# The adaLN modulation vector of a two-layer decoder step: four parts of 512 columns side by side, one set of transposes for four, and other places for the work

## The chip, the cores and the metric

The kernel runs on one core of one Trainium2 chip. The metric is the device time of one execution in microseconds (us): 1722.26 us as the median of 3 runs (1722.0 to 1723.0). One further execution was recorded by the profiler. It took 1719.56 us, and its span, from the first to the last instruction, is 1717.9 us.

## The reference, cut to what matters

One inference step of two layers: layer 0 mixes tokens by sparse attention (NSA), layer 1 by a Mamba-2 SSD scan. 512 prompt tokens and 8 sample tokens go through together, so that every activation has 520 columns. Before each mixer and each MLP there is an RMSNorm whose scale and shift, and behind it a gate, come from a conditioning vector; that is adaLN:

```python
def adaln(c, w, b):
    m = jax.nn.silu(c) @ w + b                      # c: 9 vectors of 1024, w: 1024 x 6144 per layer
    return jnp.split(m[:, None, :], 6, axis=-1)
def modulate(x, w, shift, scale):
    return rmsnorm(x, w) * (1.0 + scale) + shift

# layer i: mp = adaln(c, ada_w[i], ada_b[i])
xp = xp + mp[2] * mixer(modulate(xp, norm_w[i, 0], mp[0], mp[1]))
xp = xp + mp[5] * mlp(modulate(xp, norm_w[i, 1], mp[3], mp[4]))
```

So six pieces of 1024 numbers are wanted per layer: shift, scale and gate of the mixer, then shift, scale and gate of the MLP. All is float32.

## The kernel before, in words

All activations lie with the model dimension on the 128 partitions and the 520 tokens along the free dimension. A product of 128 output channels is 48 matmuls (8 blocks of the inner dimension, three products of split high and low halves, two halves of the columns). Its weight is one tile `w` of 128 x 1024 (512 KB), loaded by a DMA on SP's queue. ScalarE (ACT) copies it into the high half `wh` and VectorE (DVE) subtracts to get the low half; this pair is called the split of a weight here. `w` has 4 buffers, `wh` has 6. `make_plan` writes down the order in which all `w` tiles are loaded, and `get_raw` issues loads at most 4 tiles ahead of the one it hands out, so a load waits for the tile four places before it to be read.

The vector `m` of adaLN is 48 columns of 128 x 9 per layer. `ada(l, cg)` computes 4 of them, one group of 512 columns of `ada_w` (a "cg"; 12 per layer). It takes 8 matmuls: the stationary operand is the silu of the conditioning vectors, 128 x 32 per block of the inner dimension `kt`, the moving operand is a 128 x 512 block of `ada_w`, which is half of a `w` tile. A float32 matmul stands as two instructions in the trace, so these are 16 instructions. Block `kt` writes PSUM partitions `32 j` to `32 j + 32` with `j = kt % 4`: the eight blocks go round the array's four column groups, and each column group holds a partial sum of two blocks. ACT copies the 128 x 512 result (tile `ad`), four PE transposes turn it, a DVE reduce adds the four partial sums, and a DVE add puts in the bias.

Groups 0 to 3 of layer 0 are computed in `start`. The others are placed by tables:

- `attend`: groups 4 to 11 of layer 0 and 0 and 1 of layer 1. `attention` walks through 64 items (head pair, query block, head) and a tail of 6, and after each item asks a `Weaver` for `ATT_RATE` steps of other work: the sample tokens' attention (`sam_cmp`, four times `sam_branch`, `sam_fin`) and the `ada` generators, of which four stand inside a `sam_branch`, between the softmax and its transposes.
- `mlp` of layer 0: groups 3, 5, 6, 8, 9, 11 of layer 1, each run as a whole after a product named in `MLP_CGS`.
- `boundary`, between two stages: groups 2, 4 and 10. The eight matmuls stand where the norm's chain is waited for, and the reduce and the add are a `hook` in `modulated`.
- the last part of `ssd` (called the SSD's output stage here): group 7.

The output stage of `ssd` runs 8 output products `ssd_out(3, n)`, and after each one `out_fin` adds to the residual (DVE), squares (ACT) and sums the squares on GpSimd (POOL). Then the boundary to the second MLP begins: a sum over partitions by PE (`s<-c,st`), a square root, a broadcast by PE (`s<-c,r`), and the modulation.

PE, ACT, DVE, POOL and the DMA queues each run their instructions in a fixed order, which the framework's scheduler sets when the program is built.

Of the kernel before, what the change touches and what calls it, by code (L numbers as in the profile page):

```python
# [14 lines left out]
ALU = mybir.AluOpType  # L15
# [70 lines left out]
def host_inputs(x):  # L86
    c = np.ascontiguousarray
    a = {}
# [3 lines left out]
    a['ada_w'] = x['ada_w'].reshape(2, 4, 2, 128, 12, 512).transpose(0, 4, 1, 3, 2, 5).reshape(2, 12, 4, 128, 1024)  # L92
# [169 lines left out]
class Step:  # L262
# [196 lines left out]
    def load_ada(self, l, cg, whole=False):  # L459
        ws = []  # L460
        if whole:
            for kq in range(4):
                t = self.tile('wh', [128, 1024])
                self.load(t, self.I['ada_w'][l, cg, kq])
                ws += [t[:, 0:512], t[:, 512:1024]]
            return ws
        for kt in range(8):
            t = self.tile('h', [128, 512])
            self.load(t, self.I['ada_w'][l, cg, kt // 2, :, (kt % 2) * 512:(kt % 2 + 1) * 512])
            ws.append(t)  # L470
        return ws

    def ada(self, l, cg, tag='f', ws=None, fine=False):
# [18 lines left out]
        if fine:  # L492
            yield
# [80 lines left out]
    def boundary(self, tags, cg, ftag):  # L574

        ada = self.ada(1, cg, ftag, fine=True)
        for _ in range(8):
            next(ada)
        self.norm(tags, fill=ada)
        next(ada)  # L580
        h = self.modulated(lambda: next(ada))
        run_all(ada)
        return h

    def modulated(self, hook=None):
# [3 lines left out]
        for k in range(8):  # L589
            x = self.xa[k]  # L590
            self.tt(prompt(x), prompt(x), r, ALU.mult)
            if k == 0:
                self.tt(self.us, self.us, rs[:, None].to_broadcast([128, 8, 2, 4]), ALU.mult)
# [7 lines left out]
            if k == 0 and hook:  # L601
                hook()
# [519 lines left out]
    def sam_branch(self, br, k, ada):  # L1122
# [41 lines left out]
        yield from ada  # L1164
# [79 lines left out]
    def attend(self):  # L1244
        fill = [self.sam_cmp()]
        cgs = [(0, n) for n in range(4, 12)] + [(1, 0), (1, 1)]
        fill.append(self.ada(*cgs.pop(0)))
# [3 lines left out]
        fill += [self.ada(*c) for c in cgs]  # L1251
# [5 lines left out]
    def nsa_out(self):  # L1257
        h = [self.oh[i] for i in range(8)]
        self.norm_to(0, 1)
        for n in range(8):  # L1260
# [3 lines left out]
            self.scaled(n)  # L1264
        self.oh = {}
# [3 lines left out]
    def mlp(self, l, h, cgs, early=None):  # L1269
# [29 lines left out]
        for b in range(4):  # L1299
# [343 lines left out]
    def ssd(self, h):  # L1643
# [11 lines left out]
        for kind, n in SSD_SEQ:  # L1655
# [10 lines left out]
            elif kind == 'ada':  # L1666
                run_all(self.ada(1, n, 's'))
# [10 lines left out]
        fill = self.ada(1, OUT_CG, 's', fine=True)  # L1678
        for _ in range(8):
            next(fill)  # L1680
# [9 lines left out]
        run_all(fill)  # L1690
# [4 lines left out]
        self.ssd_out(3, range(2, 8))  # L1695
        self.yh = {}
        self.store(self.O['cv_p'], self.CP)
        self.store(self.O['cv_s'], self.SC)

# [44 lines left out]
    def make_plan(self):  # L1744
# [3 lines left out]
        def ada(l, *cgs):  # L1748
            for cg in cgs:
                E.extend(('ada', l, cg, k) for k in range(4))  # L1750
# [219 lines left out]
```

## Time and profile before

| | |
|---|---|
| median of 3 runs | 1722.26 us |
| the profiled execution | 1719.56 us |
| its span | 1717.9 us |
| PE busy | 1664.7 us, 97% of the span |
| DVE busy | 984.0 us, 57% |
| ACT busy | 761.6 us, 44% |
| DMA | 229.87 MB, 134 GB/s over the span |
| mean granted clock of PE | 0.993 |

The busy time of PE is the union of its matmuls; a matmul in flight counts even while the next one streams. The cost of a piece of PE work is therefore read from the timeline as the distance from its first start to the start of what follows. A view by windows gives the busy time of each engine in a stretch, the clock that was granted to PE there (1.00 is full speed, 0.50 half), and what the DMA engines moved. Of the stages, attention lies at about 208 to 431 us, the output product of the attention (`nsa_out`) at 431 to 480, the first MLP at 485 to 872, the SSD at 878 to 1333 with its output stage from about 1285, and the second MLP from 1333 to the end.

### The profile page before, as it was taken

To read this page: it belongs to the slowest core of one execution; us is meant where nothing else is said; L and a number is where in the kernel's file an instruction comes from. 1 tells how busy PE (TensorE), PEld (TensorE's weight loads), DVE (VectorE), ACT (ScalarE), POOL (GpSimd) and SP (SyncE) were. 2 spreads that over 40 slices of the span, in tenths; PEclk is the share of its full clock that TensorE was granted. 3 is DMA by queue.
4 is the path that set the end of the run, shared out by engine and by line. 5 is a ranking of instruction groups with operands and counts; after the bars stand their busy time and mean duration, and the time that the engine had idled before them with its cause. 6 is when DMAs were issued, how large, how long until landed. Compare 5 with 4: busy or idle time off the path is not lost.

```text
span 1717.9 us, 34708 instructions
## 1 busy us (share of the span) xinstructions
PE 1664.7 (97%) x13878; PEld 1538.2 (90%) x13878; DVE 984.0 (57%) x2423; ACT 761.6 (44%) x1624; POOL 143.5 (8%) x303
## 2 busy tenths in 40 slices
PE   7899999999999999999999999999998999999997
PEld 6699877667989999999989898899987999999997
DVE  2543377776464343433478968879797643434344
ACT  3534366666443131322456666646564422323231
POOL 2000112310001000000001102111022000000000
PEclk9999999999999999999999999999999999999999
DMA  8822656545433523333433442344324232323321
GB/s 302 288 87 99 215 195 223 169 148 196 137 126 97 184 87 135 99 135 136 136 135 102 135 166 90 117 135 138 125 89 160 74 99 87 96 90 93 93 86 51
DMA packets 72114, 229.87 MB, mean 134 GB/s; under 512 B 8770, under 2 KB 15218, under 8 KB 71186
## 3 DMA queue, kind: packets, MB, share of 16 engines
q1 hardware_dynamic: 62546, 198.45, 35.1%
q0 software_dynamic: 8832, 28.16, 4.5%
q8 instruction: 109, 1.79, 0.4%
q10 hardware_dynamic: 576, 1.05, 0.2%
q14 instruction: 51, 0.42, 0.1%
HBM read 204.02 MB, written 23.61 MB: 133 GB/s over the span
## 4 chain that ended last, share of the span: by engine, by line
PE 71%; DVE 8%; ACT 2%; issue 1%; POOLq 0%; DMA 0%; SPq 0%; POOL 0%; DVEq 0%; ACTq 0%
PE a L323 60%; PE s L323 5%; PE f L323 2%; PE o L323 1%; DVE wh L336 1%; PE sc L323 1%; PE t L327 1%; DVE c L345 1%; DVE g L345 1%; ACT wh L330 1%; DVE acc L336 1%; PE s L327 0%; DVE ss L1462 0%; PE f L327 0%; ACT h L333 0%
## 5 line engine op out<-in xcount | busy, mean ns | idle before, releaser
L323 PE MATMUL a<-h,wh 128*128 128x256 f32 x5952 | 743.4, 284 | 3.8 <-ACT t L333 1.6
L323 PEld LDWEIGHTS a<-h,wh 128*128 128x128 f32 x5952 | 723.3, 189 | 10.1 <-issue 3.7
L330 ACT ACTIVATE wh<-w 128x1024 fp32r<-128x1024 f32 x212 | 224.5, 1059 | 521.8 <-PE a L323 480.4
L336 DVE TENSOR_TENSOR wh<-w,wh 128x1024 fp32r<-128x1024 f32 x212 | 259.6, 1225 | 266.4 <-ACT wh L330 265.8
L323 PEld LDWEIGHTS a<-hid,wh 128*128 128x128 f32 x3072 | 370.2, 188 | 5.0 <-issue 4.2
L323 PE MATMUL a<-hid,wh 128*128 128x256 f32 (+1 forms) x3072 | 373.7, 283 | 0.0
L336 DVE TENSOR_TENSOR t<-a,c 128x8 f32<-128x8 f32 x72 | 12.0, 167 | 217.4 <-PE a L323 217.4
L323 PE MATMUL a<-yh,wh 128*128 128x256 f32 (+1 forms) x768 | 98.4, 285 | 3.0 <-DVE acc L336 1.5
L323 PEld LDWEIGHTS a<-yh,wh 128*128 128x128 f32 x768 | 93.7, 188 | 5.2 <-DVE acc L336 2.2
L330 ACT ACTIVATE hid<-t 128x520 fp32r<-128x520 f32 x64 | 40.9, 639 | 84.5 <-DVE t L336 84.5
L330 ACT ACTIVATE h<-t 128x128 f32<-128x128 f32 (+3 forms) x128 | 52.5, 440 | 46.5 <-PE t L327 46.3
L333 ACT ACTIVATE h<-sc,m 128x128 f32<-128x128 f32 (+3 forms) x128 | 66.6, 530 | 14.6 <-DVE m L340 12.5
L336 DVE TENSOR_TENSOR hid<-t,hid 128x520 fp32r<-128x520 f32 x64 | 44.7, 700 | 42.3 <-ACT hid L330 42.3
L327 PE MATMUL t<-c,h 128*128 128x128 f32 x320 | 53.5, 281 | 1.9 <-DVE h L340 0.7
L345 DVE SCALAR_TENSOR_TENSOR c<-a,c,c 128x512 f32<-128x512 f32 (+1 forms) x74 | 53.9, 728 | 1.8 <-PE a L323 1.8
L333 ACT ACTIVATE xb<-bc,x 128x128 f32<-128x128 f32 x128 | 46.4, 419 | 15.8 <-DVE xb L345 11.2
L323 PE MATMUL sc<-kv,q 128*128 128x128 f32 (+3 forms) x128 | 49.5, 387 | 0.0
L323 PEld LDWEIGHTS a<-q,wh 128*128 128x128 f32 x384 | 46.3, 188 | 1.0 <-ACT wh L330 0.8
L327 PEld LDWEIGHTS t<-c,h 128*128 128x128 f32 x320 | 34.4, 141 | 13.8 <-issue 7.7
L323 PE MATMUL a<-q,wh 128*128 128x256 f32 (+1 forms) x384 | 46.7, 283 | 0.0
L323 PE MATMUL sc<-kv,c 128*128 128x128 f32 (+3 forms) x128 | 42.3, 331 | 4.2 <-POOL c L947 4.2
L1462 DVE SCALAR_TENSOR_TENSOR ss<-ss,c,xb 128x128 f32<-128x128 f32 x128 | 43.3, 361 | 4.4 <-ACT xb L333 4.2
(366 smaller groups left out, 1941.9 us busy)
## 6 DMA issues: line engine op xcount, KB each, us to landing
w<-in_w_dram SPq DMA_DIRECT2D x128, 512.0 KB, 3.5
w<-in_ada_w_dram SPq DMA_DIRECT2D x80, 512.0 KB, 3.6
w<-in_w_ssd_dram SPq DMA_DIRECT2D x40, 512.0 KB, 3.6
w<-in_w_nsa_dram SPq DMA_DIRECT2D x20, 512.0 KB, 3.6
ss<-in_ssm_dram SPq DMA_DIRECT2D x16, 512.0 KB, 4.3
out_ssm_s_dram<-ss POOLq DMA_DIRECT2D x16, 512.0 KB, 3.0
w<-in_w_sout_dram SPq DMA_DIRECT2D x16, 512.0 KB, 4.1
cm<-in_cmp_dram SPq DMA_DIRECT2D x24, 256.0 KB, 4.0
```

Of the source, the lines that this page charges most:

```text
L323: self.nc.tensor.matmul(out, lhsT, rhs, start=start, stop=stop, skip_group_check=True)
L327: self.nc.tensor.transpose(out, in_, self.C('ident')[0:k, 0:k])
L330: self.nc.scalar.activation(out, in_, AF.Copy, **kw)
L333: self.nc.scalar.activation(out, in_, f, **kw)
L336: self.nc.vector.tensor_tensor(out, a, b, op=op)
L345: self.nc.vector.scalar_tensor_tensor(out, a, s, b, op0=op0, op1=op1, **kw)
L1462: self.nc.vector.scalar_tensor_tensor(out, a, s, b, op0=op0, op1=op1)
```

## The change: what it does

`ada` now takes two pairs of groups at once. The weight's layout in memory is changed, so that one `w` tile holds 1024 columns of one inner block `kt` (a pair of groups). For each `kt`, two tiles are fetched and four matmuls follow, one for each of four groups of 512 columns, each on a column group of its own; each column group accumulates all eight blocks. The copy to `ad` and the four transposes are done once for four groups, the reduce is gone, and the bias is added by two DVE adds that read the transposes from PSUM. `ada` stops after each `kt`, after the copy, after the transposes and at the end, 11 steps.

The places are new. In `attend` only layer 0 is left, two calls of four groups, between the branches, and `ATT_RATE` is 1.0 instead of 1.2. Layer 1's twelve groups are three calls: pairs 0 and 1 with one `kt` after each of the products 1 to 6 of `nsa_out` and the last two at the boundary to the first MLP; pairs 2 and 4 likewise over the last eight products of the first MLP and the boundary to the SSD; pairs 3 and 5 in the SSD's output stage (blocks 0 to 5) and the boundary to the second MLP. In that boundary pair 3 is the shift that the modulation adds, so `hook` stands earlier in `modulated`. The first four groups of layer 0 keep the old scheme as `ada_first`.

```diff
+    def ada(self, l, pairs, tag='f'):
         ps = self.tile(tag, [128, 512])
         for kt in range(8):
-            if ws is not None:
-                w = ws[kt]
-            else:
-                if kt % 2 == 0:
-                    raw = self.get_raw(('ada', l, cg, kt // 2))
-                w = raw[:, (kt % 2) * 512:(kt % 2 + 1) * 512]
-            j = kt % 4
-            self.mm(ps[32 * j:32 * j + 32], self.sc[:, kt, :], w, kt < 4, kt >= 4)
-            if fine or kt % 4 == 3:
-                yield
+            raw = [self.get_raw(('ada', l, a, kt)) for a in pairs]
+            for j in range(4):
+                self.mm(ps[32 * j:32 * j + 32], self.sc[:, kt, :], raw[j // 2][:, (j % 2) * 512:(j % 2 + 1) * 512],
+                        kt == 0, kt == 7)
+            yield
...
-        m = self.m[l][:, cg * 4:cg * 4 + 4, :]
-        self.nc.vector.tensor_reduce(m, p.rearrange("p t j c -> p t c j")[:, :, 0:9, :], AX.X, ALU.add)
-        b = self.adab[:, l, cg * 4:cg * 4 + 4]
-        self.tt(m, m, b[:, :, None].to_broadcast([128, 4, 9]), ALU.add)
+        yield
+        for n, a in enumerate(pairs):
+            b = self.adab[:, l, 8 * a:8 * a + 8].rearrange("p (j t) -> p t j", t=4)
+            self.tt(self.m[l][:, 8 * a:8 * a + 8, :].rearrange("p (j t) c -> p t j c", t=4),
+                    p[:, :, 2 * n:2 * n + 2, 0:9], b[:, :, :, None].to_broadcast([128, 4, 2, 9]), ALU.add)
...
-        for br, k in SAM_ORDER:
-            fill.append(self.sam_branch(br, k, self.ada(*cgs.pop(0))))
+        for (br, k), pairs in zip(SAM_ORDER, ((2, 4), (3, 5), None, None)):
+            if pairs:
+                fill.append(self.ada(0, pairs))
+            fill.append(self.sam_branch(br, k))
...
-                if (b, n) in cgs:
-                    run_all(self.ada(1, cgs[b, n]))
+                if ada and b == 3 and n in ADA_AT:
+                    next(ada)
...
-        fill = self.ada(1, OUT_CG, 's', fine=True)
-        for _ in range(8):
+        fill = self.ada(1, (3, 5), 's')
+        for _ in range(2):
             next(fill)
...
-        run_all(fill)
+        for _ in range(2):
+            next(fill)
...
-        self.ssd_out(3, range(2, 8))
+        for n in (2, 4, 6):
+            self.ssd_out(3, (n, n + 1))
+            if n < 6:
+                next(fill)
...
-MLP_CGS = {(0, 2): 3, (0, 6): 5, (1, 2): 6, (2, 2): 8, (2, 6): 9, (3, 3): 11}
+ADA_AT = {1: 0, 2: 1, 3: 2, 4: 3, 5: 4, 6: 5}
...
-ATT_RATE = 1.2
+ATT_RATE = 1.0
```

The order on PE in the first MLP before, at the first group there (`a` is a product's PSUM tile, `f` the adaLN sum, `w` its weight; a row with x2 is two matmuls):

```order
L323 MATMUL f_7721<-w_7544,c_101 32x512 x2
L323 MATMUL f_7721<-w_7603,c_101 32x512 x2
L323 MATMUL f_7721<-w_7662,c_101 32x512 x2
L323 MATMUL f_7721<-w_7722,c_101 32x512 x2
...
L327 MATMUL f_7740<-c_72,ad_7738 128x128 x4
```

And now, in `nsa_out`, at the first two of the six places:

```order
L323 MATMUL a_6213<-q_6102,wh_6138 128x264
L323 MATMUL f_6272<-w_6135,c_101 32x512 x2
L323 MATMUL f_6272<-w_6141,c_101 32x512 x2
L323 MATMUL a_6287<-q_2980,wh_6143 128x256
...
L323 MATMUL f_6272<-w_6273,c_101 32x512 x2
L323 MATMUL f_6272<-w_6275,c_101 32x512 x2
L323 MATMUL a_6360<-q_2980,wh_6209 128x256
```

Eight matmuls in one piece and four transposes became pieces of four matmuls, one after each product, with no transposes between products.

The order on PE in the SSD's output stage before, at the broadcast of the SSD's own norm (`s<-c,r`; `a` is a product's PSUM tile):

```order
L323 MATMUL a_16805<-yh_16239,wh_16604 128x264
L323 MATMUL a_16805<-yh_16238,wh_16605 128x256
L323 MATMUL s_16756<-c_72,r_16753 128x128 x4
L323 MATMUL s_16730<-c_72,r_16753 128x8
L327 MATMUL s_16767<-c_72,xd_16765 128x128 x4
L323 MATMUL a_16805<-yh_16238,wh_16605 128x264
L323 MATMUL a_16805<-yh_16488,wh_16604 128x256
```

And now, from the same broadcast to the sixth output product (`s_16561` is the adaLN sum):

```order
L323 MATMUL s_16596<-c_72,r_16593 128x128 x4
L323 MATMUL s_16570<-c_72,r_16593 128x8
L323 MATMUL s_16561<-w_16503,c_101 32x512
L323 MATMUL s_16561<-w_16505,c_101 32x512 x2
L323 MATMUL s_16561<-w_16507,c_101 32x512 x2
...
L323 MATMUL s_16561<-w_16509,c_101 32x512 x2
...
L323 MATMUL s_16561<-w_16515,c_101 32x512 x2
...
L323 MATMUL s_16561<-w_16517,c_101 32x512 x2
...
L323 MATMUL s_16561<-w_16718,c_101 32x512 x2
L323 MATMUL s_16561<-w_16720,c_101 32x512 x2
```

The four transposes gave way to blocks 2 to 5, and the scheduler has cut the blocks into unequal pieces between and within the products.

The order on DVE in the same stage before (`acc<-acc,a` takes a product in, `acc<-acc,z` scales it, `wh<-w,wh` is the low half of a weight's split):

```order
L336 TENSOR_TENSOR acc_12906<-acc_12906,a_16683 128x520
L336 TENSOR_TENSOR wh_16680<-w_16671,wh_16679 128x1024
L336 TENSOR_TENSOR acc_12933<-acc_12933,a_16684 128x520
L336 TENSOR_TENSOR wh_16802<-w_16673,wh_16801 128x1024
L495 TENSOR_REDUCE c_100<-s_16767 128x36
L336 TENSOR_TENSOR acc_12906<-acc_12906,z_16762 128x520
L336 TENSOR_TENSOR c_100<-c_100,c_88 128x36
...
L336 TENSOR_TENSOR wh_16882<-w_16675,wh_16881 128x1024
...
L336 TENSOR_TENSOR wh_16962<-w_16677,wh_16961 128x1024
```

And now:

```order
L336 TENSOR_TENSOR acc_12738<-acc_12738,a_16523 128x520
L336 TENSOR_TENSOR acc_12765<-acc_12765,a_16524 128x520
L336 TENSOR_TENSOR acc_12738<-acc_12738,z_16602 128x520
...
L336 TENSOR_TENSOR acc_12798<-acc_12798,a_16644 128x520
L336 TENSOR_TENSOR wh_16520<-w_16511,wh_16519 128x1024
...
L336 TENSOR_TENSOR wh_16641<-w_16513,wh_16640 128x1024
...
L336 TENSOR_TENSOR wh_16729<-w_16638,wh_16728 128x1024
...
L336 TENSOR_TENSOR wh_16817<-w_16726,wh_16816 128x1024
```

Before, two splits stood ahead of the scaling and two among the later products; now all four stand among the products, and the reduce and its add are gone from here.

## Rows read from the trace of the kernel before

**Rows 1.** The page, part 1: busy time, share of the span and instructions of each engine.

```profile
PE 1664.7 (97%) x13878; PEld 1538.2 (90%) x13878; DVE 984.0 (57%) x2423; ACT 761.6 (44%) x1624; POOL 143.5 (8%) x303
```

**Rows 2.** By windows: window, length, busy (instructions) of each engine, PE's clock, DMA share, GB/s.

```profile
34.00:64.00 30.00, 24.54 (x183) 15.35 (x182) 10.91 (x31) 11.91 (x19) 2.80 (x6) 1.00 0.99 357
...
209.00:345.00 136.00, 129.56 (x1227) 92.02 (x1226) 101.92 (x369) 87.02 (x279) 36.80 (x95) 0.99 0.59 202
345.00:420.00 75.00, 72.88 (x650) 51.06 (x650) 54.47 (x204) 48.95 (x157) 9.20 (x27) 1.00 0.46 167
...
440.00:480.00 40.00, 39.42 (x329) 37.77 (x327) 18.34 (x41) 16.23 (x23) 0.00 (x0) 1.00 0.32 93
...
485.00:872.00 387.00, 385.71 (x3207) 374.00 (x3205) 166.50 (x280) 124.96 (x167) 8.05 (x15) 1.00 0.37 122
```

**Rows 3.** Timeline of PE, first MLP: start, length, instructions.

```profile
561.35 1.92 PE L323 MATMUL f<-w,c 128*32 128x512 f32 x16
563.20 0.98 PE L323 MATMUL a<-hid,wh 128*128 128x256 f32 x6
564.02 0.65 PE L327 MATMUL f<-c,ad 128*128 128x128 f32 x4
564.43 22.60 PE L323 MATMUL a<-hid,wh 128*128 128x256 f32 x186
```

**Rows 4.** Timeline of PE, attention.

```profile
358.96 1.07 PE L323 MATMUL f<-w,c 128*32 128x512 f32 x8
359.95 0.44 PE L323 MATMUL sc<-kv,q 128*128 128x384 f32 x1
...
361.37 0.60 PE L327 MATMUL f<-c,ad 128*128 128x128 f32 x4
361.72 0.48 PE L323 MATMUL sc<-kv,q 128*128 128x512 f32 x1
```

**Rows 5.** By tile `ad`: one copy to it for each adaLN group outside the SSD.

```profile
L330 ACT ACTIVATE ad<-f x22: 572/598/616, 39.0 to 872.3; 128x512 f32<-128x512 f32 x22
```

**Rows 6.** Timeline of PE, SSD's output stage; in brackets idle time and who ended it.

```profile
1287.48 1.90 PE L323 MATMUL s<-w,c 128*32 128x512 f32 x10
1289.32 2.42 PE L323 MATMUL a<-yh,wh 128*128 128x256 f32 x18
1291.67 1.06 PE L323 MATMUL s<-w,c 128*32 128x512 f32 x6
1292.66 1.28 PE L323 MATMUL s<-c,yss 128*128 128x1 f32 x10
...
1311.59 5.98 PE L323 MATMUL a<-yh,wh 128*128 128x256 f32 x48 [1.44 <-DVE c L336]
...
1324.71 2.19 PE L323 MATMUL s<-c,st 128*128 128x1 f32 x10 [4.05 <-POOL st L534]
...
1333.22 14.50 PE L323 MATMUL a<-h,wh 128*128 128x256 f32 x96 [0.36 <-ACT h L333]
1348.40 11.79 PE L323 MATMUL a<-h,wh 128*128 128x256 f32 x96 [0.67 <-ACT t L333]
```

**Rows 7.** Timeline of DVE, the same stage.

```profile
1314.95 1.21 DVE L336 TENSOR_TENSOR wh<-w,wh 128x1024 fp32r<-128x1024 f32 x1
```

**Rows 8.** By windows, the same stage.

```profile
1320.00:1325.00 5.00, 0.95 (x6) 0.29 (x3) 4.93 (x10) 1.90 (x5) 3.08 (x2) 0.99 0.99 391
1325.00:1330.00 5.00, 4.42 (x21) 4.33 (x22) 0.28 (x2) 2.16 (x4) 0.00 (x0) 0.50 0.06 24
```

**Rows 9.** Timeline of PE, boundary between attention and first MLP.

```profile
480.02 1.28 PE L323 MATMUL t<-c,ssq 128*128 128x1 f32 x10 [0.60 <-DVE ssq L336]
...
484.57 0.63 PE L323 MATMUL a<-h,wh 128*128 128x256 f32 x3 [1.25 <-ACT h L333]
```

**Rows 10.** DMA issues: what, queue, count, KB each, median us from issue to landing.

```profile
w<-in_ada_w_dram SPq DMA_DIRECT2D x80, 512.0 KB, 3.6
...
wh<-in_ada_w_dram SPq DMA_DIRECT2D x4, 512.0 KB, 7.2
```

More of the change, by code (lines that the diff above doesn't have):

```diff
@@ L455, in first_products, with load_ada @@
         return ps
-    def load_ada(self, l, cg, whole=False):
+    def load_ada(self, cg, whole=False):
         ws = []
[L461 to L466, printed above, removed]
-        for kt in range(8):
-            t = self.tile('h', [128, 512])
-            self.load(t, self.I['ada_w'][l, cg, kt // 2, :, (kt % 2) * 512:(kt % 2 + 1) * 512])
+        for kt in range(8):
+            if not whole:
+                t = self.tile('h', [128, 512])
+            elif kt % 2:
+                t = u[:, 512:1024]
+            else:
+                u = self.tile('wh', [128, 1024])
+                t = u[:, 0:512]
+            self.load(t, self.I['ada_w'][0, cg // 2, kt, :, (cg % 2) * 512:(cg % 2 + 1) * 512])
@@ L470, in load_ada, with ada_first @@
             ws.append(t)
         return ws
-    def ada(self, l, cg, tag='f', ws=None, fine=False):
+    def ada_first(self, cg, ws):
+        ps = self.tile('f', [128, 512])
+        for kt in range(8):
+            j = kt % 4
+            self.mm(ps[32 * j:32 * j + 32], self.sc[:, kt, :], ws[kt], kt < 4, kt >= 4)
+        s = self.tile('ad', [128, 512])
+        self.copy(s, ps)
+        p = self.tile('f', [128, 4, 4, 32])
+        for t in range(4):
+            self.tr(p[:, t].rearrange("p j c -> p (j c)"), s[:, t * 128:(t + 1) * 128])
+        m = self.m[0][:, cg * 4:cg * 4 + 4, :]
+        self.nc.vector.tensor_reduce(m, p.rearrange("p t j c -> p t c j")[:, :, 0:9, :], AX.X, ALU.add)
+        b = self.adab[:, 0, cg * 4:cg * 4 + 4]
+        self.tt(m, m, b[:, :, None].to_broadcast([128, 4, 9]), ALU.add)
@@ L572, in norm, with boundary @@
         self.r = next(r)
-    def boundary(self, tags, cg, ftag):
-        ada = self.ada(1, cg, ftag, fine=True)
-        for _ in range(8):
+    def boundary(self, tags, ada):
+        for _ in range(2):
             next(ada)
@@ L592, in modulated @@
             if k == 0:
+                if hook:
+                    hook()
                 self.tt(self.us, self.us, rs[:, None].to_broadcast([128, 8, 2, 4]), ALU.mult)
@@ L600, in modulated @@
             out.append((hi, lo))
-            if k == 0 and hook:
-                hook()
         self.xa = []
@@ L1264, in nsa_out, with mlp @@
             self.scaled(n)
+            if n in ADA_AT:
+                next(ada)
         self.oh = {}
-    def mlp(self, l, h, cgs, early=None):
+    def mlp(self, l, h, ada=None, early=None):
         hid = {}
@@ L1307, in mlp @@
                 second(b, n)
-                if (b, n) in cgs:
-                    run_all(self.ada(1, cgs[b, n]))
+                if ada and b == 3 and n in ADA_AT:
+                    next(ada)
             if l == 1 and b == 3:
@@ L1689, in ssd @@
         self.vcopy(sample(self.ry), rs)
-        run_all(fill)
+        for _ in range(2):
+            next(fill)
         for n in range(2):
@@ L1698, in ssd @@
         self.store(self.O['cv_s'], self.SC)
+        return fill
     def last(self, l, hid):
@@ L1746, in make_plan, with ada @@
         E = []
-        def ada(l, *cgs):
-            for cg in cgs:
-                E.extend(('ada', l, cg, k) for k in range(4))
+        def ada(l, pairs, kts=range(8)):
+            E.extend(('ada', l, a, k) for k in kts for a in pairs)
         def w(*key):
@@ L1757, in make_plan, with mlp @@
         E.append('stop')
-        cgs = [(0, n) for n in range(4, 12)] + [(1, 0), (1, 1)]
-        ada(*cgs.pop(0))
         for n, (br, k) in enumerate(SAM_ORDER):
+            if n < 2:
+                ada(0, ((2, 4), (3, 5))[n])
             for j in range(4):
                 w('selk' if br == 1 else 'wink', 4 * k + j)
-            ada(*cgs.pop(0))
-        for c in cgs:
-            ada(*c)
         for n in range(8):
             w('w_nout', n)
-        def mlp(l, cgs):
+            if n in ADA_AT:
+                ada(1, (0, 1), (ADA_AT[n],))
+        def mlp(l):
             for n in range(8):
@@ L1777, in mlp @@
                     w('w2', l, b, n)
-                    if (b, n) in cgs:
-                        ada(1, cgs[b, n])
+                    if l == 0 and b == 3 and n in ADA_AT:
+                        ada(1, (2, 4), (ADA_AT[n],))
                 if b < 3:
@@ L1792, in make_plan @@
                 if n == 3:
-                    ada(1, OUT_CG)
+                    ada(1, (3, 5), range(4))
                 for k in range(4):
                     w('w_sout', 4 * n + k)
-            elif kind == 'ada':
-                ada(1, n)
+                    if n == 3 and k in (1, 2):
+                        ada(1, (3, 5), (3 + k,))
             elif kind != 'pair':
                 w('w_ssd', o + (kind == 'z'))
-        ada(1, BOUND_CGS[2])
-        mlp(1, {})
+        ada(1, (3, 5), (6, 7))
+        mlp(1)
         E.append('stop')
@@ L1935, in ssd_seq @@
             out.append(('out', g - 1))
-        if q in SSD_CGS:
-            out.append(('ada', SSD_CGS[q]))
         out.append(('z', q))
```

50 lines of the change are left out of this document (20 added, 30 removed).

## The prediction

> **What bounds the kernel now.** I read the busy shares first: PE is busy for 97% of the span and no other engine passes 57% [rows 1]. An average over stages can hide one with another limit, so the windows come next. In the first MLP PE is busy 385.71 of 387 us, in the output product of the attention 39.42 of 40 us, in attention 129.56 of 136 and 72.88 of 75 us [rows 2]. In these stages an instruction taken from PE shortens the stage and one put in lengthens it, as long as no new wait comes. The timeline then shows the exception, the SSD's output stage: PE sits idle 1.44 us for DVE and 4.05 us for POOL before the last sum over partitions [rows 6], while DVE is busy 4.93 of 5 us. Behind that gap the granted clock falls from 0.99 to 0.50 [rows 8], the lower of PE's two levels, 1.2 GHz instead of 2.4.
>
> One expectation has to go first. Four column groups at once is not new: before, the eight blocks of a group already went round the four column groups. Eight matmuls stay 16 instructions, and the total of matmuls stays as it was. What goes is transposes (and copies and reduces on other engines); what changes is where the matmuls stand.
>
> **The change part by part.** The sum is made against the profiled execution of 1719.56 us; the median is 2.7 us above it, and the difference is then taken from the median.
>
> *Six whole groups leave the first MLP.* One stands in rows 3: from 561.35 to 564.43 is 3.08 us. In it are six product instructions, at 22.60 / 186 = 0.12 us each, 0.73 us. The group costs PE 2.35 us, with its transposes and with no idle time. Six of them: -14.1 us.
>
> *Twelve pieces of four matmuls come in between products*, six in the attention's output product and six in the MLP's last block. Such a piece (8 instructions) stands in the attention: from 358.96 to 359.95, 0.99 us [rows 4]. Twelve: +11.9 us. One piece of 16 took 561.35 to 563.20, 1.85 us [rows 3], so cutting it in two costs 0.13 us.
> The Trainium skill's page "TensorEngine Tiling (Array Packing)", section Key Properties, says that a change of the tiling mode drains the array. That speaks against many small pieces. Without a drain a piece would be half of 1.85 us and the sum below 0.8 us better; the rows side with the page, and the sum goes by the rows.
>
> *Attention* loses two of ten groups, four pieces, -4.0 us, and eight of ten sets of transposes at 361.72 - 361.37 = 0.35 us [rows 4], -2.8 us. (The copies to `ad` count the groups: 22, and two more in the SSD [rows 5].) Where two pieces ran as one before, the 0.13 us comes back: at most ten times, 1.3 us, and I take 0.4 us. The other engines lose only work. But these groups also filled PE's waits for the softmax, and the last items now have no fill: counted by the generators' stops, 81 steps at a rate of 1.2 lasted for nearly all 70 items, and 63 steps at 1.0 end seven items early. PE's idle time in the two windows is 6.44 + 2.12 = 8.6 us [rows 2]. The loss of cover lies between 0 and half as much again, 4 us. I take 1.5 us, since the item's own matmuls remain and the chain from scores to transposes has two items' time.
>
> *The SSD's output stage* gets the matmuls of two more groups. The order shows the pieces: five matmuls behind the broadcast, then 2, 2, 2 and 4, and one ahead of it. A piece of five took 1287.48 to 1289.32, 1.84 us, because a column group came round twice; one of three took 0.99 us [rows 6], like one of four. So 1.84 + 5 x 0.99 - 0.35 for the transposes that go = +6.4 us of PE. The products ended at 1311.59 + 5.98 = 1317.6; with the 1.44 us filled, now 1322.5, and 1324.4 with the boundary's piece of eight matmuls. The end of the stage was not PE's, though: it was DVE's chain at 1324.71. On DVE the order puts all four splits behind the first product that is added, where two stood before: two more at 1.21 us [rows 7], 1327.1, +2.4 us. (Bounds: 0 if they fall into a wait, and +6.4 if PE became the bound.) PE then waits some 2.7 us, and in two parts, since the last adaLN weight loads into the buffer of a tile whose split is the fourth; before, it was 4.05 us in one.
> The likelier case is that the clock then stays up. From the last sum to the first product of the second MLP it was 1333.22 - 1324.71 = 8.5 us. At full clock the boundary behind attention took 484.57 - 480.02 = 4.55 us [rows 9]; here a second set of sums comes to it, half of 2.19 or 1.1 us, and two adds of the hook, which now stand ahead of the first modulated block, 0.4 us (bounds 0 and 1.21, another DVE instruction's length): 6.1 us, -2.4 us. The next 96 matmuls took 14.50 us, and the 96 behind them 11.79: -2.7 us. Stage: 2.4 - 2.4 - 2.7 = -2.7 us.
>
> *At nothing:* the hooks of the other two boundaries (their adds are not needed by that modulation), the first four groups (four more loads in a window whose DMA engines are 0.99 busy anyway [rows 2]; a wait there would cost at most their issue), and the loads between products, three tiles in some 6.8 us against 3.6 us for one to land [rows 10].
>
> Sum: -14.1 + 11.9 - 6.8 + 0.4 + 1.5 - 2.7 = -9.8 us: 1709.8 us for a profiled execution, **1712.5 us** for the median.
>
> **The rivals.** *The clock falls again in the output stage.* For it: PE still has a gap before the last sum, and the new pieces wait for their weights one after the other. Against it: the gap is shorter and broken by matmuls, and gaps of 0.60 and 1.25 us at the other boundary [rows 9] left the MLP behind it at full clock [rows 2]. Then the stage is +2.4 + 0.4 = +2.8 us, and the sum -4.3 us: 1718.0 us.
> The Trainium skill's page "TensorE: Matmul & The Clock Gate", section HAM oscillation, has this as a rule: waits for DMA between short bursts of matmuls let the clock fall, so a filled gap need not keep it up. The trace has one fall, behind one gap of 4.05 us, and doesn't settle it.
>
> *The weights come late in attention: slower.* An adaLN step there now takes two tiles (1.05 MB) at every item; before, a group's four tiles were spread over four steps of its own and the branch around it. By the stage times under the table an item took (431 - 208) / 70 = 3.2 us; with a step now some 3.7 us (an estimate: half of the step's 0.99 us on top, since the fill of before goes). PE runs in order, so a step whose tile is not there holds the scores of the next item and everything behind them. With four buffers a tile has two steps less one piece, 2 x 3.7 - 1.0 = 6.4 us, to land. For the rival: 283 GB/s would be wanted where 202 were moved, and at the start, with the engines 0.99 busy, a tile took 7.2 us. Against it: the median for these tiles is 3.6 us [rows 10], and 357 GB/s have been reached [rows 2]. Sixteen steps are eight pairs, each waiting for what exceeds 6.4 us: at 7.2 us +6.4 us, 1718.9 us; from 8.1 us on the kernel is slower by over 0.2%; at 9 us +20.8 us, 1733 us.
>
> *The cover was worth more:* if the idle time of attention doubles, +8.6 instead of +1.5 us, the sum is -2.7 us: 1719.6 us.
>
> **How the numbers follow.** About 0.2% (3.4 us) is what a measurement can tell from no change: faster is under 1718.8 us, slower over 1725.7. Forecast 0.55; the clock falls 0.27; late weights 0.09; the lost cover 0.09. The forecast's own range: with no loss of cover and no delay by the splits -13.7 us, with 4 us lost and one wait of 1.5 us more -5.8: 1708.5 to 1716.5. The clock's fall and the lost cover reach to 1720; what is left out above is the late weights, and below a little: 1707.5 to 1720.5. Faster: 0.55, half of 0.27, and a little of the rest: 0.74. Same: the other half, the cover, and late weights at their mildest: 0.17. Slower: 0.09.
>
> **What would show it.** In the first MLP no `f` row until its last block, and the stage (with its boundary) shorter by 8 us. In the output product, pieces of 8 instructions at 0.99 us, stage longer by 6 us. In attention, 16 pieces at 0.99 us, the stage shorter by some 5 us, and no wait for `in_ada_w_dram` in the view of waits over 1 us; such waits, at a median landing above 6.4 us, would be the slower rival. In the output stage the last sum near 1327 on the old scale, and behind it either a clock of 1.00 and 96 matmuls in 11.8 us, or 0.50 and 14.5. I am wrong if pieces between products cost much more than 1 us, or if attention doesn't shorten.

## The result and the profile after

The changed kernel took **1731.82 us** in the median (9 runs, 1730.34 to 1747.15) where before took 1722.26 (9 runs beside them, 1720.44 to 1725.76): ratio 1.0079, 95% interval 1.0050 to 1.0108. The forecast was 1712.5. The change made the kernel slower, for the larger part in a way that no rival of the prediction described.

The profiled execution after is one of 1736.19 us (span 1734.5, mean granted clock 0.986; before 1719.56, 1717.9 and 0.993). Its stages, by the start of the first instruction of each on TensorE:

| stretch (us) | before | after | difference | forecast |
|---|---|---|---|---|
| to the attention's first scores | 208.41 | 210.64 | +2.2 | 0 |
| attention, to the first output product | 222.41 | 227.29 | +4.9 | -4.9 |
| output product, to the norm's sums | 49.20 | 56.11 | +6.9 | +5.9 |
| boundary | 4.55 | 4.55 | 0 | 0 |
| first MLP, to its norm's sums | 388.03 | 383.11 | -4.9 | -8.2 |
| boundary and SSD, to its first output product | 412.64 | 413.76 | +1.1 | 0 |
| output stage, to the last sum | 39.47 | 43.71 | +4.2 | +2.4 |
| from there to the second MLP | 8.51 | 9.33 | +0.8 | -2.4 |
| second MLP | 384.7 | 386.0 | +1.3 | -2.7 |

Each column is one execution. Second profiles of the same kernels (b0 of before, a0 of the changed one, both under the experiments) show how far a stage moves by itself: before's output stage took 40.58 us in b0, its first MLP 388.98; the changed kernel's attention took 225.41 us in a0, and its start 208.72.

Part 1 of the page, beside [rows 1]: PE is busy 18.9 us longer, with 60 instructions fewer; DVE and ACT are busy for less, POOL for 2.7 us more.

```profile
PE 1683.6 (97%) x13818; PEld 1543.8 (89%) x13818; DVE 976.8 (56%) x2393; ACT 753.5 (43%) x1609; POOL 146.2 (8%) x303
```

By windows of the same stages (columns as in [rows 2]): attention in two parts, output product, first MLP.

```profile
209.00:347.00 138.00, 132.65 (x1153) 88.03 (x1155) 91.72 (x333) 80.69 (x257) 24.54 (x65) 0.98 0.60 216
347.00:425.00 78.00, 75.39 (x659) 52.67 (x656) 58.46 (x202) 50.65 (x156) 22.07 (x59) 1.00 0.43 132
445.00:493.00 48.00, 48.00 (x392) 40.96 (x390) 18.79 (x42) 16.99 (x23) 0.00 (x0) 1.00 0.58 209
499.00:881.00 382.00, 380.72 (x3133) 373.08 (x3134) 162.90 (x268) 121.42 (x163) 8.04 (x15) 0.99 0.34 108
```

PE is as busy in the attention as before, 132.65 + 75.39 of 216 us against 129.56 + 72.88 of 211 [rows 2]. Its granted clock is nearly the same, 0.98 and 1.00 in the two parts against 0.99 and 1.00. So the stage is longer by work of PE, not by waits. The view of lines with shapes kept apart says which: line, operation, out<-in, count, then busy us and mean ns of one, idle time before it. Before, attention only:

```profile
L323 PE MATMUL f<-w,c 128*32 128x512 f32 x160 | 21.6, 603 | 0.1
L323 PE MATMUL f<-w,np 128*32 128x512 f32 x64 | 9.6, 598 | 0.7 <-DMA w<-in_selk_dram 0.7
L327 PE MATMUL f<-c,ad 128*128 128x128 f32 x40 | 6.1, 275 | 0.2 <-ACT ad L330 0.2
```

And after:

```profile
L323 PE MATMUL f<-w,c 128*32 128x512 f32 x128 | 20.3, 605 | 0.9 <-DMA w<-in_ada_w_dram 0.8
L323 PE MATMUL f<-w,np 128*32 128x512 f32 x64 | 17.4, 599 | 0.0
L327 PE MATMUL f<-c,ad 128*128 128x128 f32 x8 | 1.2, 272 | 0.0
```

The transposes `f<-c,ad` went as foreseen, 40 to 8. The adaLN matmuls `f<-w,c` lost a fifth of their instructions and only 1.3 us. And the 64 instructions of `f<-w,np` cost 7.8 us more, with the same mean length of one. These are not adaLN's: they are the scores of the sampled rows in `sam_branch`, and the change doesn't touch these matmuls. They cost more because fewer of them run side by side; the next section shows it.

The pieces between products came out at the price that was forecast; here two in the output product (timeline of PE):

```profile
449.68 1.07 PE L323 MATMUL f<-w,c 128*32 128x512 f32 x8
450.67 6.05 PE L323 MATMUL a<-q,wh 128*128 128x256 f32 x48
456.65 1.06 PE L323 MATMUL f<-w,c 128*32 128x512 f32 x8
```

A piece is 450.67 - 449.68 = 0.99 us, as in [rows 4].

### The profile page after: what moved, and what is told of

It reads as the page before. It is cut to its first block, busy times and chain, and to the rows that moved or that the text cites. A ratio compares the mean times of both kernels' runs of the same rounds, so it can differ in the third digit from the quotient of the medians.

```text
span 1734.5 us, 34555 instructions
## 1 busy us (share of the span) xinstructions
PE 1683.6 (97%) x13818; PEld 1543.8 (89%) x13818; DVE 976.8 (56%) x2393; ACT 753.5 (43%) x1609; POOL 146.2 (8%) x303
## 4 chain that ended last, share of the span: by engine, by line
PE 68%; DVE 7%; ACT 2%; issue 1%; POOLq 0%; DMA 0%; DVEq 0%; POOL 0%; ACTq 0%
PE a L323 60%; PE s L323 5%; DVE wh L336 1%; PE f L323 1%; PE o L323 1%; ACT wh L330 1%; DVE c L345 1%; DVE g L345 1%; DVE ss L1473 0%; DVE acc L336 0%; PE s L327 0%; PE t L327 0%; PE sc L323 0%; DVE xb L345 0%; DVE xd L336 0%
## 5 line engine op out<-in xcount | busy, mean ns | idle before, releaser
L323 PE MATMUL a<-h,wh 128*128 128x256 f32 (+1 forms) x5952 | 746.1, 285 | 4.5 <-ACT h L333 2.3
L323 PEld LDWEIGHTS sc<-kv,q 128*128 128x128 f32 x128 | 24.9, 195 | 25.0 <-issue 20.2
```

What stands on the lines that cost most here:

```text
L323: self.nc.tensor.matmul(out, lhsT, rhs, start=start, stop=stop, skip_group_check=True)
```

## Why the attention grew: the scores of the sampled rows

The filler of the attention is a chain of generators; a credit of so many steps an item decides which steps fall into which item of the attention. `sam_branch` issues its scores in two steps, blocks 0 and 1, then 2 and 3, and block i writes column group i. At a rate of 1.2, steps and items come round together every 6 steps (5 items), and a branch with its adaLN group has 12: the two score steps met in one item in all four branches. On PE they stood in one piece in three of them; in the fourth a late weight (0.74 us for `in_selk`) parted them into 10 and 6 instructions. At a rate of 1.0 an item takes one step, so they never meet.

Timeline of PE, before, third branch; 16 instructions on four column groups:

```profile
307.55 1.94 PE L323 MATMUL f<-w,np 128*32 128x512 f32 x16
309.41 0.49 PE L323 MATMUL sc<-kv,q 128*128 128x512 f32 x1
```

After, first branch; twice 8 instructions, each on two column groups:

```profile
274.03 1.91 PE L323 MATMUL f<-w,np 128*32 128x512 f32 x8
275.88 0.39 PE L323 MATMUL sc<-kv,q 128*128 128x256 f32 x1
...
276.95 1.91 PE L323 MATMUL f<-w,np 128*32 128x512 f32 x8
278.80 0.44 PE L323 MATMUL sc<-kv,q 128*128 128x384 f32 x1
```

Sixteen took 309.41 - 307.55 = 1.86 us, eight take 1.85 us: half the work for the same time. Before, three branches took 1.94 us each and the parted one 3.8; now there are eight halves at 1.91, and two of them are cut once more, 1.04 us each. That is the 7.8 us. That a column group works beside the others is what the Trainium skill's page "TensorEngine Tiling (Array Packing)" says under Key Properties; the rows agree, and show the other side of it: a group without work is not made up for.

## The experiments

The run time of every kernel here moves with its mean granted clock, and the kernels were timed on several chips, each group of them beside runs of before; the ratios are to these. Runs of before, of several chips, spread from 1715.6 to 1737.7 us, with clocks of 0.994 down to 0.979. A line through all runs, with one slope and an offset for each kernel, has a slope of 1.42 ± 0.07 us for 0.001 of clock, and the runs scatter about it by 2.0 us (a ± is a 95% interval here). The table gives the plain median and ratio, and the offset against before at equal clock (0.990), which tells differences of work and waits apart from those of the clock. Two things limit it. It was taken up only after e1 to e4 had been timed, so their expectations speak of plain times. And it leaves out what a kernel does to the clock: in nine of the ten groups of runs with the change in them (e4 is the exception) the mean clock was below that of before beside them, by 0.001 to 0.004.

| kernel | median, runs | ratio, 95% interval | mean clock | at equal clock, us |
|---|---|---|---|---|
| before | 1723.62, 110 | 1 | 0.9876 | 0 |
| changed | 1731.82, 9 | 1.0079, 1.0050 to 1.0108 | 0.9866 | +9.5 ± 0.9 (both) |
| changed, again | 1737.46, 12 | 1.0072, 1.0043 to 1.0101 | 0.9858 | |
| e1 scores in one step | 1733.67, 12 | 1.0049, 1.0019 to 1.0079 | 0.9832 | +3.7 ± 1.2 |
| e2 before, shifted | 1726.79, 12 | 0.9994, 0.9973 to 1.0016 | 0.9907 | +5.4 ± 1.2 |
| e3 blocks 2 to 5 left out | 1736.54, 12 | 1.0038, 1.0010 to 1.0067 | 0.9854 | +6.4 ± 1.2 |
| e4 = e1, double pieces | 1727.43, 12 | 1.0010, 0.9983 to 1.0037 | 0.9867 | +2.2 ± 1.2 |
| e5 = e4, later weights first | 1728.66, 12 | 1.0016, 0.9991 to 1.0041 | 0.9859 | +0.4 ± 1.2 |
| e6 = e5, pieces early | 1731.99, 12 | 1.0043, 1.0008 to 1.0078 | 0.9841 | +3.4 ± 1.2 |
| e7 = e5, blocks in the tail | 1729.99, 12 | 1.0031, 1.0006 to 1.0056 | 0.9845 | +1.1 ± 1.2 |
| e8 = e5, blocks spread | 1728.96, 12 | 1.0039, 1.0012 to 1.0066 | 0.9846 | +0.1 ± 1.2 |
| e9 = e5, rate 0.9 | 1726.32, 12 | 1.0004, 0.9982 to 1.0027 | 0.9863 | -0.9 ± 1.2 |
| e10 = e9, earlier pieces | 1730.26, 12 | 1.0037, 1.0007 to 1.0066 | 0.9852 | +2.6 ± 1.2 |

The second group of runs of the changed kernel (a0) was expected at 1730 to 1732 us at clock 0.990, and is at 1731.6 there.

In the profiles the longest stretches at the lower clock that differ between executions lie at the start of the attention, ahead of its first adaLN block. PE waits there for POOL's masks. In 13 of the 14 profiles, of before too, the wait was 1.6 to 2.9 us and the clock fell to 0.50 in it or just behind it, for very different times; in a0 it was 1.0 us and the clock stayed up. Before had 0.66 at 215 to 220 us and 1.00 from then on. e3 had 0.50 from 215 to 240, with PE busy all the time, and its attention took 239.65 us, where a0's, with the same work, took 225.41. Two windows of 5 us, of a0 and of e6:

```profile
225.00:230.00 5.00, 5.00 (x48) 3.92 (x46) 4.06 (x14) 4.79 (x15) 0.58 (x2) 1.00 0.01 3
```

```profile
225.00:230.00 5.00, 5.00 (x33) 3.59 (x32) 0.40 (x2) 1.78 (x5) 0.29 (x1) 0.50 0.00 0
```

Why the low stretch is short in one execution and long in another stays open.

**e1, the scores in one step again.**

```diff
-            if j % 2:  ...  yield          # after j = 1 and j = 3
+        ...  yield                         # once, after j = 3
```

> The changed kernel with one edit: in sam_branch the score matmuls of the first and second half of a branch are issued in one step again (the generator yields after them once, not twice). Theory A (the attention's missing gain is the scores' two column groups: a step of 8 instructions on two groups takes 1.85 to 1.9 us, as much as 16 on four): the 64 score instructions f<-w,np fall from 16.7 us back to about 9.3, the attention stage from 227.3 to about 220, the run from 1731.8 to about 1724.5 (ratio to before 1.001 to 1.003). Rival B (the loss lies in the lost cover and in the clock at the attention's start and in the output stage): the time stays within 1.5 us of the changed kernel, 1730 to 1733.

At equal clock e1 is 5.8 ± 1.4 us below the changed kernel: near theory A's 7.3 and far from rival B's 1.5. By the plain median it isn't below it (1733.67 us against 1731.82), and its ratio, 1.0049, lies above the 1.001 to 1.003 that theory A gave. The trace shows the step itself: the scores are whole again in three branches (in the third they took 3.78 us), and the 64 are busy for 9.6 us, as before:

```profile
272.74 1.94 PE L323 MATMUL f<-w,np 128*32 128x512 f32 x16
```

The attention only fell from 227.29 to 226.22 us and not to 220: PE now waited 3.8 us for `in_ada_w` (0.8 in after; e5 and e8 below) and 5.8 us for POOL's masks (2.8), and the clock was 0.97 there (0.98). The plain median shows no gain because e1's mean clock was 0.0034 lower in its 12 runs, worth 4.8 us by the line.

**e2, before with the filler shifted by one step.**

```diff
-        fill = [self.sam_cmp()]
+        fill = [iter([None]), self.sam_cmp()]
```

> The kernel before with one edit: the filler of the attention gets one empty step in front, so that every later step falls one step later among the attention's items; no work is added or removed. Theory A: the two score steps of each of the four branches then fall into different items (by the order of PE they stand in pieces of 4 and 4 matmuls in place of 8), the 64 score instructions go from 9.3 us to about 16.7, and the kernel before gets slower by about 7 us, to about 1729. Rival B: a shift by one step changes nothing but noise, within 1.5 us of 1722.3.

The attention of before grew from 222.41 to 226.95 us, with no instruction more and at the same granted clock of 0.99. The 64 score instructions were busy for 15.6 us, where they had been for 9.6. Timeline of PE, third branch:

```profile
310.97 1.91 PE L323 MATMUL f<-w,np 128*32 128x512 f32 x8
312.81 0.50 PE L323 MATMUL sc<-kv,q 128*128 128x512 f32 x1
...
314.77 1.91 PE L323 MATMUL f<-w,np 128*32 128x512 f32 x8
```

At equal clock it costs 5.4 ± 1.2 us, somewhat less than the 7 of theory A, since no half was cut once more here. The plain ratio says no change: e2's mean clock was 0.0031 above that of all runs of before, worth 4.4 us, and why it held better is not explained. So the plain times show neither e1's gain nor e2's loss. At equal clock, and in the rows of the scores themselves, the price of the split is shown twice, by taking it away and by adding it.

**e3, the output stage without four blocks' matmuls.**

```diff
+            for j in range(0 if kt in (2, 3, 4, 5) else 4):     # pairs (3, 5) of layer 1
```

> The changed kernel, with the adaLN matmuls of blocks 2 to 5 of the pairs (3, 5) left out on TensorE in the SSD's output stage; their weights are still loaded, and the sums of these two parts are then incomplete. If TensorE's time sets the end there (theory P: four pieces of 1.85 us make the stage 43.7 us long where it was 39.5), the stage falls by 5 to 7 us and the run to about 1725. If the chain of VectorE does (theory D, that of the prediction: two more splits ahead of the last products), the stage stays above 42 and the run gains less than 1.5 us. If the late last weights do (theory W: w<-in_ada_w waited 1.73 us at the last piece), it gains 1.7 us or less plus what follows it.

The stage fell from 43.71 to 40.52 us, the run by 3.1 ± 1.4 at equal clock (by the plain median it didn't fall): between P and D. Timeline of PE in e3 at the stage's end (a view ends with its window, so the last row of a fence can hold fewer instructions than ran):

```profile
1330.30 3.11 PE L323 MATMUL a<-yh,wh 128*128 128x256 f32 x24 [1.36 <-DVE c L336]
1333.83 3.13 PE L323 MATMUL a<-yh,wh 128*128 128x256 f32 x24 [0.43 <-DVE acc L336]
...
1342.52 1.38 PE L323 MATMUL s<-w,c 128*32 128x512 f32 x4 [2.88 <-DMA w<-in_ada_w_dram]
1344.63 0.59 PE L323 MATMUL s<-c,st 128*128 128x1 f32 x2 [0.73 <-POOL st L546]
```

With the pieces gone PE waits for DVE again, and for the last weights: DVE's chain and the loads alone need 40.5 us, and PE's pieces add the 3.2 us above it. That is 1.1 us more than in the first profile of before, but no more than in two others of its order of work: b0 took 40.58 us and e2 40.60, both with the clock at 0.91 in the stage's first half. So by these profiles a delay by DVE's two splits is at most 1.1 us, and may be none.

**e4, pieces of two blocks (on e1).**

```diff
-ADA_AT = {1: 0, 2: 1, 3: 2, 4: 3, 5: 4, 6: 5}
+ADA_AT = {1: (0, 1), 3: (2, 3), 5: (4, 5)}
```

> The kernel of e1 with the pieces between products doubled: two blocks at once after products 1, 3 and 5 (in the SSD's output stage two blocks at each of three places) in place of one block at six places. Theory C (each return to a product of 128 columns costs about 0.13 us, as the prediction had it, and nothing else changes): 9 returns fewer, about 1.2 us less than e1. Rival (a double piece needs four buffers of weights at once, with four there are, so the next weights can be asked for only after it): waits on w<-in_ada_w of 0.5 to 2 us at most of the nine places, 3 to 10 us more than e1.

Against e1 -1.5 ± 1.6 us at equal clock: the size of theory C, not proven by the timing. The output product fell from 56.12 to 55.28 us for three pieces fewer, 0.28 us each and so twice theory C's 0.13, and no piece between products waited.

**e5, the column groups of the later half first (on e4).**

```diff
-            for j in range(4):
+            for j in (2, 3, 0, 1):
```

> The kernel of e4, with the four column groups of a block issued in the order 2, 3, 0, 1, so that the half whose weights land later goes first and a block is not cut in two by the scheduler: by the order of PE the 32 matmuls of pairs (3, 5) in the output stage stand in pieces of 7, 1, 3, 1, 4, 4, 4 and 8, where e4 has 5, 3, 1, 5, 2, 2, 2, 2, 2 and 8. Theory E (a piece on two column groups takes as long as one on four, about 1 us, so the cuts are what made s<-w,c cost 12.5 us and not 7.6): s<-w,c falls by 2 to 3.5 us, the output stage from 44 to about 41.5 and the run by about 2.5 us against e4 at the same clock (1722 at 0.990). Rival (DVE or the loads set that stage's end, as e3 hints, whose stage with half the blocks left out was still 40.5): the stage stays above 43.3 and the run within 1 us of e4.

Against e4 -1.85 ± 1.6, against e1 -3.3 ± 1.6 us. The time of `s<-w,c`, from start to next start, in the output stage fell from 12.5 (after; 13.3 in e4) to 9.7 us, by fewer cuts. The stage itself stayed, at 44.27 us where e4 had 44.07: the time turned into waits, here for the weights and for POOL's end of DVE's chain:

```profile
1313.67 1.07 PE L323 MATMUL s<-w,c 128*32 128x512 f32 x8 [1.94 <-DMA w<-in_ada_w_dram]
...
1334.11 1.05 PE L323 MATMUL s<-c,st 128*128 128x1 f32 x8 [3.37 <-POOL st L547]
```

So in that stage theory E has the piece's price right and the rival the stage; what e5 gained, it gained elsewhere (in the attention, for one, no adaLN block is cut in two any more).

**e6 and e10, the pieces further ahead of the boundary (on e5, on e9).** e6 puts them after products 0, 1, 2 in both places, e10 after 1, 2, 3 in the output product alone.

> The kernel of e5 with the pieces between products moved from after products 1, 3, 5 to after 0, 1, 2, in the attention's output product and in the last part of the first MLP, so that five whole products stand between the last piece and the boundary. Theory F (the clock fell to 0.50 behind boundary 0 in all four profiles of kernels with pieces, and in neither of before's, because the stretch ahead of the gap holds pieces): the granted clock is 1.00 through both boundaries, worth about 3 us at boundary 0 and 1 to 2 at boundary 1; the run's mean clock is 0.002 higher than e5's. Rival (the fall there is by chance, or set by something else): falls there as often as in e1 and e4. A double piece right behind another may wait for weights, 0.5 to 2 us each, which the profile would show apart.

> The kernel of e9 with the three double pieces of the attention's output product moved from after products 1, 3, 5 to after 1, 2, 3, so that four products stand between the last of them and boundary 0 (the scheduler cuts two of them in two, two more returns of 0.13 us); nothing else is moved. Theory F: the clock stays at 1.00 behind boundary 0, as in e6, worth 1.7 us (e9 spent 490 to 500 at 0.66), less 0.3 us for the returns; at equal mean clock the time does not differ, the mean clock is 0.001 higher. Rival: it falls there as in e9.

Both slower, by 3.1 ± 1.6 and 3.5 ± 1.6 us at equal clock. In e6 the clock stayed up behind boundary 0 and fell behind boundary 1; in e10 it fell behind both. Theory F falls. e10's pieces waited for weights in four places, 2.3 us in all; for e6 only 0.9 us of its loss is seen in the output product, the rest is open.

**b0, before once more.**

> The kernel before, unaltered, for a second profile of it: does the clock fall behind the boundaries (at 480 and 873) belong to the change? In eight of the nine profiles of kernels with pieces ahead of boundary 0 the granted clock fell behind it; in that of before and of e2 (before, shifted) it did not. Theory F: no fall there this time either. Rival (it falls there by chance in any kernel): one fall or more at the two boundaries.

(Of the ten profiles with pieces that there were by then, nine had fallen.) The clock fell behind boundary 0, in a kernel without a piece between products. Windows of before's first and of its second profile, the last three columns clock, DMA share and GB/s:

```profile
480.00:485.00 5.00, 3.53 (x27) 3.11 (x28) 2.12 (x8) 2.60 (x7) 0.00 (x0) 1.00 0.94 380
485.00:490.00 5.00, 4.66 (x39) 4.44 (x38) 5.00 (x13) 3.27 (x8) 0.00 (x0) 1.00 0.09 36
```

```profile
480.00:485.00 5.00, 4.17 (x24) 3.63 (x24) 1.33 (x6) 1.95 (x4) 0.00 (x0) 0.67 0.96 391
485.00:490.00 5.00, 4.64 (x26) 4.48 (x26) 5.00 (x14) 3.11 (x10) 0.00 (x0) 0.65 0.06 19
```

So the 3.2 us that the first MLP lost behind its boundary in the profile after is nothing that only the change brings. Whether it makes such falls likelier (10 of 11 profiles with pieces, 1 of 3 without) stays open.

**e7, two blocks behind the last product (on e5).**

> The kernel of e5 with blocks 4 and 5 of the pairs (3, 5) moved from between the output stage's products to behind them, ahead of the norm's sums, where before waited 4.05 us for POOL. Theory G (time between the products of this stage is on the path, the tail is not): the last sum stands 1.5 to 2 us earlier than in e5 and waits for POOL under 0.5 us, the run 1.5 us shorter. Rival (the weights of blocks 6 and 7 can be asked for only when 4 and 5 free their buffers, 3.6 to 4.1 us from issue to landing): a wait on w<-in_ada_w of 1.5 to 3 us in the tail, and the run the same or up to 2 us longer.

The last sum came 2.9 us earlier in its stage (41.35 us), more than theory G had, but it still waited 3.85 us for POOL, where theory G had under 0.5. And the scheduler put the last two blocks into the norm's broadcast, where each took 1.9 us at a clock of 0.50: from the last sum to the second MLP it took 14.04 us where e5 took 8.10. In all 0.8 ± 1.6 us more: moved, not gained.

**e8 and e9, more time for the weights in the attention (on e5).** e8 alternates blocks of pairs (3, 5) with the steps of the branch ahead of them; e9 sets `ATT_RATE = 0.9`.

> The kernel of e5 with the second group of the attention, pairs (3, 5) of layer 0, no longer in eight steps one behind the other, but one block alternating with one step of the branch in front of it: the same work in another order. Theory H (what e5 still lacks against the forecast in the attention is late weights: w<-in_ada_w waits 5.4 us in two places there, 3.9 of them at 305, and the DMA engines are full at 300 to 310): with a block every second item the waits fall under 1 us, the fall of the clock behind them goes, and the run comes out 4 to 5 us below e5 at the same clock, about 1718 at 0.990 where before has 1722. Rival (the wait moves to another load or to POOL, which e5 waited for 3.1 us in this stretch): within 1.5 us of e5's 1722.3.

> The kernel of e5 with the filler's rate in the attention 0.9 steps an item in place of 1.0. Theory H: each block has 11% more time for its weights, so the 5.4 us of waits fall by about a half, 2 to 3 us; but the schedule then has one branch whose scores are cut into 1 and 7, which takes 1 us back: 1720 to 1721 at clock 0.990. Rival: the filler ends later and leaves steps for the end, where they stand bare: 2 to 4 us slower than e5.

Their reason is e5's wait, and the clock behind it (timeline of PE; two windows):

```profile
305.23 1.94 PE L323 MATMUL f<-w,c 128*32 128x512 f32 x8 [3.92 <-DMA w<-in_ada_w_dram]
```

```profile
300.00:305.00 5.00, 1.31 (x12) 0.91 (x8) 1.81 (x6) 1.62 (x7) 2.25 (x6) 0.97 0.99 373
305.00:310.00 5.00, 4.77 (x22) 2.78 (x24) 1.53 (x7) 0.47 (x2) 1.56 (x4) 0.50 1.03 363
```

That is the prediction's slower rival, the late weights, in a kernel whose scores take all four buffers in one step; in the changed kernel itself these waits were 0.8 us, and late weights showed as blocks cut in two (below). The Trainium skill's page "TensorE: Matmul & The Clock Gate", section HAM oscillation, has this pattern, a wait for DMA between matmuls and a low clock behind it; the windows agree here (0.50), and the boundaries above show that the same short gap may or may not do it.

In e8 the wait moved, as its rival said: 1.5 us for `in_ada_w`, but 3.3 for `in_selk` and 7.9 for POOL's masks, where e5 had 6.2; -0.2 ± 1.6 us. In e9 the first two rows of its waits in the attention are

```profile
PE sc L323 <- POOL c L959: 6.8, 7, 1.9
PE f L323 <- DMA w<-in_ada_w_dram: 2.1, 3, 1.2
```

(5.4 for `in_ada_w` in e5), and it gains 1.25 ± 1.6 us, the size that theory H gave it, not proven. e9 is the best of the variants: 10.4 ± 1.4 us below the changed kernel at equal clock, and level with before (ratio 1.0004, 0.9982 to 1.0027). No version here beats before.

## Why the prediction was wrong

**First MLP: right.** Summed from each start to the next, the adaLN matmuls of the stage gave back 4.6 us, the transposes 2.4, the products `a<-hid,wh` 0.6 and a wait 0.6: -8.2, the forecast. Against it stand 3.2 us in `a<-h,wh`, at the lower clock behind the boundary. In e5 the stage is 7.3 us shorter.

**Pieces between products: right in price, the return left out.** 0.99 us each, as forecast. Six in the output product came to +6.9 and not +5.9: the products themselves were 0.94 us longer, 0.16 for each time that one was left and taken up again. The prediction's 0.99 us runs from a piece's start to the next product matmul's, so what it costs the product is not in it. Its 0.13 us for cutting one piece in two is another price, and is in the 0.99 already. What either price consists of, no run here shows, so the prediction's "the rows side with the page" goes too far.

**Attention: the step that failed.** "Attention loses two of ten groups ... and eight of ten sets of transposes", with a loss of cover of 1.5 us, counted adaLN's own instructions and the waits. The transposes went, and the cover mattered little: PE's waits between 200 and 440 us were 9.1 us before and 8.5 after. What the working left out is that the generators and the rate, which it did count for the stage's length, also decide which steps stand together. The scores' two halves came apart in all four branches: +7.8 us of busy time, 5.8 by e1, 5.4 by e2. A smaller part is the adaLN blocks cut in two by their weights' arrival: 128 instructions were busy for 20.3 us (21.7 in a0), where 16 whole pieces at the 1.06 us for which one is busy would be 17.0. This is the rival of the late weights, in another form than it was written: 0.8 us of waits and 3.3 us of cuts. By the prediction's own sign, that attention doesn't shorten, it was wrong.

**Output stage: mis-sized, and with another bound.** DVE's chain was forecast at +2.4 us and measured +1.1 at most with PE's pieces out of the way (e3). But PE became the bound, the case that stood only in the brackets:

```profile
1319.68 1.05 PE L323 MATMUL s<-w,c 128*32 128x512 f32 x4
1320.66 5.39 PE L323 MATMUL a<-yh,wh 128*128 128x264 f32 x43
1325.99 1.07 PE L323 MATMUL s<-w,c 128*32 128x512 f32 x8
1326.98 5.99 PE L323 MATMUL a<-yh,wh 128*128 128x256 f32 x48
...
1336.54 1.05 PE L323 MATMUL s<-w,c 128*32 128x512 f32 x4 [1.73 <-DMA w<-in_ada_w_dram]
1339.17 1.01 PE L323 MATMUL s<-c,st 128*128 128x1 f32 x4 [1.57 <-POOL st L546]
```

Four instructions cost 1320.66 - 1319.68 = 0.98 us, eight 1326.98 - 1325.99 = 0.99: a block cut in two costs two pieces. Products and pieces ran without a gap up to the last weights, and the 4.05 us wait of [rows 6] shrank to 1.73 + 1.57. The stage took +4.2 us, or +3.1 against b0.

**The clock behind it: the first rival was right.** It fell, as before [rows 8]:

```profile
1335.00:1340.00 5.00, 1.89 (x8) 0.98 (x9) 4.79 (x10) 1.74 (x3) 2.41 (x2) 0.87 1.03 397
1340.00:1345.00 5.00, 4.42 (x21) 4.33 (x22) 0.33 (x2) 2.46 (x4) 0.00 (x0) 0.50 0.27 108
```

Two gaps with a short piece between them did no better than one, so the -2.4 and -2.7 us of the forecast are gone. The prediction's "one fall" in the trace of before was not the only one either: at 215 to 220 us the clock was 0.66, behind the 2.8 us wait at the attention's start.

**The sum.** With the first rival's clock the prediction had -4.3 us. At equal clock the changed kernel is 9.5 us above before (by the plain ratios, 1.0079 and 1.0072, 12 to 14). Of the 14 between, e1 accounts for 5.8 and the steps to e9 for 4.6 together; the output stage (+1.8 over its term) and the returns lie partly in these. Some 3 us are not located by an experiment. In the profiled execution another 2.2 us stand before the attention and 3.2 behind the first boundary, both under a lowered clock.

## What to carry to other kernels

When work is taken out of a chain that an interleaver deals out by a rate, list where every other step of the chain now falls, and above all which steps ran side by side only because they fell together: write such pairs as one step. Price a piece by how often its fullest column group comes round (here 0.98 us for once, 1.85 for twice), not by its matmuls, and see whether its loads arrive together. And where runs move with the granted clock, compare kernels at equal clock and by stage, beside the plain medians.

## What was not expected of the hardware

- Eight instructions on two column groups took 1.85 us, as long as sixteen on four (1.86); four took 0.98, eight on four groups 0.99. Six pieces between products made the products 0.94 us longer.
- Behind the same short gaps (0.60 and 1.25 or 1.00 us) of the same kernel the granted clock stayed at 1.00 in one execution and was 0.67 and 0.65 in another. Runs of before lay up to 22 us apart along their mean clock, 1.42 us for each 0.001.
- With PE busy 5.00 of 5 us in every window from 215 to 240 us the granted clock of e3 stayed at 0.50; in a0 it was 1.00 in the same windows.
